# Two transformer blocks in split fp32: a third seven-product K pair in each FFN gemm, its weight sums made by an adding DMA

## The chip, the cores and the metric

The kernel runs on one core of a Trainium2 chip. The metric is the device time of one execution in microseconds (us), the median of several runs. The difference between two kernels is what counts; both compute the same function of the same inputs.

## The reference, cut to what matters

One sequence of S = 256 tokens with D = 2048 features passes through two blocks in float32, B = 1. Nearly all of the arithmetic is matrix products with weights that are used once:

```
# block 1
h = rmsnorm(x);  proj = h @ w_in                   # 2048 -> 6144
x = x + concat(dilated_attention, diff_attention) @ w_out
h = rmsnorm(x)
x = x + (silu(h @ w_gate) * (h @ w_up)) @ w_down   # 2048 -> 2 x 5632 -> 2048
x = rmsnorm(x)
# block 2
z = rmsnorm(x) @ w_in_2                            # 2048 -> 10256
merged = g_a * (fox_attention @ w_proj_a) + g_m * (mlstm @ w_proj_m)
x = x + merged @ w_out_2
u = causal_dwconv(rmsnorm(x) @ w_up_2, conv_w, conv_b)   # 2048 -> 11264
x = x + (silu(u_gate) * u_val) @ w_down_2          # 5632 -> 2048
```

## The kernel before

**Products in split fp32.** TensorE multiplies in a reduced fp32 format (F32R). Each fp32 operand is split into a high part and a low part in that format, and a product is hi·hi + hi·lo + lo·hi, three matmuls (`mm3`, L131 to L134, or L137 and L138 where the weights are the stationary operand). A weight tile goes one way through the engines: SP issues its DMA into a tile `raw` (L70, 128 x 2048, 1 MB, 3 buffers), ScalarE (ACT) casts 1024 columns of it to `wh` (L80), VectorE (DVE) subtracts to get `wl` (L81), and TensorE (PE) uses both. `wh` and `wl` have 4 buffers each.

**Gemms.** The function `gemm` (L167) makes 256 x 1024 outputs in four PSUM banks `c[t][n]`, a token half by a column half, and walks over "K pairs", 256 rows of the weight at a time. A plain pair is a 2 x 2 by 2 x 2 block product: 8 products of three matmuls with 512 columns, 24 matmuls. The first `n_sum` pairs of a gemm are done with seven products instead (a Strassen-Winograd scheme): 21 matmuls. For those, sums of blocks stand in the place of blocks. The sums of the activations are made once per pair (`sums`, L118: four 128 x 128 operations on GpSimd (POOL), a cast on ACT and a subtraction on DVE). The sums of the weights are made for each gemm: `ta` (L187, one DVE operation 128 x 1024) and `tb` (L188 and L189). After the seven-product pairs the extra banks p1, p5, p6, p7 are combined into four tiles `plus` (L212 to L216), which are added to the outputs: by POOL in `add_blocks` (L253), where the output goes into the residual, or by DVE in `block` (L243).

**Stages.** The norms' row factors are applied late, so that products can start without them. The first stage takes the transposed input `xin` from HBM, splits it (L105 to L111) and multiplies (`xstat`, L151), while POOL squares `xin` for the first norm (L403 to L410). Then come attention, the output gemms `wo1`, the squares of the residual (`sq_add`) and the transposes of the residual back into stationary form (`resid_pairs`, L289, by L263). The first FFN has three parts of 3, 4 and 4 gate-up gemms (8 K pairs each, weights `wgu`), and each part ends in two down gemms (`wd`) of 6, 8 and 8 K pairs. The second block's FFN does its up products with `conv` (L919, by `wstat`, L140) and its down gemms `wd2` in the same three parts; the row factor there is broadcast over partitions by a matmul (`bcast`, L350) at its start. Seven-product pairs stand in 11 gate-up, 6 `wd` and 6 `wd2` gemms, N_SUM = N_SUMD = 2 of them in each: 46.

**Order.** The code is not the order of the instructions: a scheduler with modelled times puts each engine's instructions in a row. On each engine they then run in that row, each waiting for the semaphores of what it reads and of the buffers it writes.

## Time and profile before

| | |
|---|---|
| median of 3 runs | 2576.76 us (2575.09 to 2577.85) |
| profiled execution | 2575.72 us |
| its span | 2573.8 us |
| TensorE busy | 2530.7 us, 98% of the span |
| weight loads of TensorE | 81% |
| VectorE busy | 71% |
| ScalarE busy | 52% |
| GpSimd busy | 7% |
| mean HBM rate | 184 GB/s |

The span is the time between the first and the last instruction of the profiled execution; 1.9 us of the measured time lie around it. A busy share is a mean over stages with different limits. Matmuls are pipelined, so that a matmul is shown as lasting 0.39 us although the next one starts 0.23 us after it: what a matmul costs is read from start to start. "Idle before", in square brackets, is the time in which an engine stood idle ahead of an instruction, with what ended it.

### The profile page before, as it was taken

The numbers are of one execution on the slowest core, as the hardware profiler recorded it, in microseconds if no ns is written. First come the engines' busy times: TensorE is split into PE (matmuls) and PEld (weight loads), VectorE is DVE, ScalarE is ACT, GpSimd is POOL, SyncE is SP. The second block draws the span as 40 slices with busy tenths as digits, with TensorE's granted clock in tenths as the row PEclk, the third lists the DMA queues.
The fourth block names the chain that finished last, engine by engine and source line by source line (L and its number), as shares of the span: only waits on it lengthen the run. The fifth ranks groups of instructions, "written<-read, shape, count | busy, mean of one in ns | idle before, by whom it ended". The sixth has DMA issues, their size and how long they took to land. (4 is left out here: it accounts for less than half of the span.)

```text
span 2573.8 us, 31105 instructions
## 1 busy us (share of the span) xinstructions
PE 2530.7 (98%) x12050; PEld 2094.5 (81%) x12050; DVE 1821.8 (71%) x2354; ACT 1340.8 (52%) x1882; POOL 167.3 (7%) x125
## 2 busy tenths in 40 slices
PE   7999999999999999999999999999899999999999
PEld 6888887878878888777888888888788888888887
DVE  6666556789778877877566555455589887878796
ACT  4555555555555454546455644444455455545553
POOL 3000000102101100110000000000000100110011
PEclk9999999999999999999999999999999999999999
DMA  7444444545545555554544455555455655555554
GB/s 273 152 158 170 171 164 158 190 176 198 209 167 210 180 210 170 197 196 165 195 161 154 176 180 188 189 195 180 154 190 180 210 183 185 192 196 184 193 178 166
DMA packets 66244, 472.60 MB, mean 184 GB/s; under 512 B 7345, under 2 KB 7601, under 8 KB 9777
## 3 DMA queue, kind: packets, MB, share of 16 engines
q1 hardware_dynamic: 65520, 468.53, 51.8%
q8 instruction: 94, 1.54, 0.2%
q10 hardware_dynamic: 576, 2.10, 0.2%
q14 instruction: 54, 0.43, 0.0%
HBM read 468.50 MB, written 2.10 MB: 183 GB/s over the span
## 5 line engine op out<-in xcount | busy, mean ns | idle before, releaser
L81 DVE TENSOR_TENSOR wl<-raw,wh 128x1024 fp32r<-128x1024 f32 (+1 forms) x882 | 1082.4, 1234 | 597.3 <-ACT wh L80 596.1
L80 ACT CAST wh<-raw 128x1024 fp32r<-128x1024 f32 (+1 forms) x882 | 902.0, 1029 | 995.1 <-PE d L134 649.5
L133 PE MATMUL d<-wl,x 128*128 128x512 f32 x1532 | 599.6, 393 | 11.6 <-DVE wl L81 11.6
L134 PE MATMUL d<-wh,x 128*128 128x512 f32 x1532 | 597.9, 392 | 0.0
L132 PE MATMUL d<-wh,x 128*128 128x512 f32 x1532 | 572.1, 394 | 3.4 <-ACT wh L80 3.2
L137 PE MATMUL a<-x,wh 128*128 128x512 f32 x1536 | 542.0, 398 | 0.0
L138 PE MATMUL a<-x,wl 128*128 128x256 f32 x1536 | 431.6, 281 | 0.0
L133 PEld LDWEIGHTS d<-wl,x 128*128 128x128 f32 x1532 | 288.4, 188 | 74.8 <-DVE wl L81 15.2
L137 PEld LDWEIGHTS a<-x,wh 128*128 128x128 f32 x1536 | 289.0, 188 | 70.1
L132 PEld LDWEIGHTS d<-wh,x 128*128 128x128 f32 x1532 | 287.1, 188 | 67.1 <-ACT wh L80 8.2
L134 PEld LDWEIGHTS d<-wh,x 128*128 128x128 f32 x1532 | 288.6, 188 | 59.1 <-DVE x L116 0.5
L138 PEld LDWEIGHTS a<-x,wl 128*128 128x128 f32 x1536 | 290.9, 189 | 0.2
L133 PE MATMUL d<-wl,y 128*128 128x512 f32 x624 | 242.2, 391 | 0.0
L134 PE MATMUL d<-wh,y 128*128 128x512 f32 x624 | 241.5, 390 | 0.0
L132 PE MATMUL d<-wh,y 128*128 128x512 f32 x624 | 217.3, 392 | 0.1
L133 PEld LDWEIGHTS d<-wl,y 128*128 128x128 f32 x624 | 117.1, 188 | 27.0 <-DVE wl L81 2.3
L132 PEld LDWEIGHTS d<-wh,y 128*128 128x128 f32 x624 | 116.5, 188 | 25.8 <-ACT wh L80 2.2
L134 PEld LDWEIGHTS d<-wh,y 128*128 128x128 f32 x624 | 117.2, 188 | 24.0
L81 DVE TENSOR_TENSOR wl<-ta,wh 128x1024 fp32r<-128x1024 f32 x46 | 56.2, 1223 | 46.6 <-ACT wh L80 46.6
L132 PE MATMUL a<-wh,y 128*128 128x512 f32 x216 | 83.4, 392 | 3.2 <-DVE x L111 3.2
L134 PE MATMUL a<-wh,y 128*128 128x512 f32 x216 | 84.4, 392 | 0.0
L133 PE MATMUL a<-wl,y 128*128 128x512 f32 x216 | 84.4, 391 | 0.0
(335 smaller groups left out, 2418.9 us busy)
## 6 DMA issues: line engine op xcount, KB each, us to landing
raw<-in_wgu SPq DMA_DIRECT2D x88, 1024.0 KB, 4.8
raw<-in_wd SPq DMA_DIRECT2D x88, 1024.0 KB, 4.8
raw<-in_wup SPq DMA_DIRECT2D x88, 1024.0 KB, 4.8
raw<-in_w SPq DMA_DIRECT2D x47, 1024.0 KB, 4.8
raw<-in_wo SPq DMA_DIRECT2D x32, 1024.0 KB, 4.8
raw<-in_wgs SPq DMA_DIRECT2D x32, 1024.0 KB, 4.8
raw<-in_wfox SPq DMA_DIRECT2D x24, 1024.0 KB, 4.8
raw<-in_wpr SPq DMA_DIRECT2D x16, 1024.0 KB, 4.8
```

What stands on the lines that cost most here:

```text
L80: act.copy(wh[:, :n], src)
L81: dve.tensor_sub(wl[:, :n], src, wh[:, :n].bitcast(F32))
L132: pe.matmul(ps, ah, wh, start=start, stop=False)
L133: pe.matmul(ps, ah, wl, start=False, stop=False)
L134: pe.matmul(ps, al, wh, start=False, stop=stop)
L137: pe.matmul(ps, wh, pr.t[:, :, j, :], start=start, stop=False)
L138: pe.matmul(ps[:, 0:S], wl, pr.hi(j), start=False, stop=stop)
```

## The change

- **Three seven-product pairs per gemm.** N_SUM and N_SUMD go from 2 to 3, 69 seven-product pairs in place of 46.
- **First weight sums by DMA.** L187 is gone. SP issues a plain DMA that writes the block b12 twice into `ta` (128 x 2 x 512, 512 KB written), and then GpSimd issues a DMA that reads the blocks b11 and b22 from HBM (512 KB) and adds them to what stands in `ta`. Both are issued for up to three seven-product pairs ahead (`ta_ahead`), over gemm bounds, into 3 buffers. The host lays the weights out as b11, b22, b12, b21, so that each DMA reads contiguous columns.
- **No elementwise work of these kinds on GpSimd.** The four operations in `sums` go to DVE. The squares of the first norm go to ACT, which reads the untransposed input `xn` (two squares of 128 x 2048). The tiles `plus` are added to the residual by DVE, ahead of the gemm's last pairs (`fold`). GpSimd keeps the 69 adding DMAs and the 8 additions of L896.
- **Pairs in turns.** In a gemm, a seven-product pair takes turns with a plain pair: `one`, the plain pair's first half, `two`, its second half, `three`. The chain that makes `plus` comes right after the last seven-product pair, and the last pair goes bank by bank.
- **Smaller raw tiles.** 128 x 1024 with 7 buffers in place of 128 x 2048 with 3: 966 rows of SP in place of 457.
- **Order around the stages.** The residual's transposes for one half of the columns are asked for right after that half's gemm, ahead of the squares. In the second FFN four `conv` products are started, half by half, ahead of the norm's row factor. A few PSUM banks and temporary tiles change places and numbers.

```diff
-N_SUM = 2
-N_SUMD = 2
-TT_BUFS = 1
+N_SUM = 3
+N_SUMD = 3
+TA_BUFS = 3
+TB_BUFS = 1
+BY_COL = ((0, 0), (1, 0), (0, 1), (1, 1))
...
-    rp = ctx.enter_context(tc.tile_pool(name="rp", bufs=3))
+    rp = ctx.enter_context(tc.tile_pool(name="rp", bufs=7))
...
-            pool.tensor_sub(f[:, 0], a21, a22)
-            pool.tensor_sub(f[:, 2], a11, a21)
-            pool.tensor_sub(f[:, 1], f[:, 0], a11)
-            pool.tensor_add(f[:, 3], a12, f[:, 1])
...
+            dve.tensor_sub(f[:, 0], a21, a22)
+            dve.tensor_sub(f[:, 2], a11, a21)
+            dve.tensor_sub(f[:, 1], f[:, 0], a11)
+            dve.tensor_add(f[:, 3], a12, f[:, 1])
...
+    def ta_ahead(k):
+
+        while len(given) < min(len(jobs), k + 3):
+            src = jobs[len(given)]
+            ta = sx.tile([P, 2, 512], F32, tag="ta", name="ta", bufs=TA_BUFS)
+            nc.sync.dma_start(ta, src[:, 1024:1536].unsqueeze(1).to_broadcast([P, 2, 512]))
+            given.append(ta)
+            if len(given) > 1:
+                ta_add()
+        while len(added) < min(len(jobs), k + 2):
+            ta_add()
+
+    def ta_add():
+        n = len(added)
+        pool.dma_start(given[n], jobs[n][:, 0:1024].rearrange("p (a b) -> p a b", a=2), accum_op=ALU.add)
+        added.append(n)
...
+            def load(self):
+                ta_ahead(len(taken))
+                self.ta = given[len(taken)]
+                taken.append(self.i)
+                self.r = [raw_tile(srcs[self.i][:, 0:1024]), raw_tile(srcs[self.i][:, 1536:2048])]
+                self.tb = sx.tile([P, 2, 512], F32, tag="tb", name="tb", bufs=TB_BUFS)
+
+            def sum_b(self):
+                dve.tensor_add(self.tb[:, 0], self.ta[:, 0], self.r[0][:, 512:1024])
+                dve.tensor_add(self.tb[:, 1], self.tb[:, 0], self.r[1][:, 0:512])
...
+            def two(self):
+                later(lambda: self.cut(2, self.ta.rearrange("p a b -> p (a b)"), 1024))
+                mm(p5, lambda: self.lhs(0), self.w[2], 0)
+                mm(p7, lambda: self.lhs(2), self.w[2], 512)
...
+        n_with = min(n_sum, max(0, len(plains) - tail))
+        if not n_sum:
+            n_with = 0
+        for i, sv in enumerate(sevens):
+            pl = plains[i] if i < n_with else None
+            later(sv.load)
+            if pl:
+                later(pl.load)
+            if pl is None:
+                later(sv.sum_b)
+            sv.one()
+            if pl:
+                later(lambda pl=pl: pl.cut(0, dve))
+                later(lambda pl=pl: pl.cut(1, dve))
+                later(sv.sum_b)
+                pl.part(0)
+            sv.two()
+            if pl:
+                pl.part(1)
+            sv.three()
...
-    def add_blocks(c, plus, g):
-
-        for t in range(2):
-            for n in range(2):
-                o = g * 1024 + n * 512
-                r = resid[:, t, o:o + 512]
-                if plus is not None:
-                    pool.tensor_add(r, r, plus[t][n])
-                dve.tensor_add(r, c[t][n], r)
+    def add_blocks(c, g):
+
+        for t, n in BY_COL:
+            o = g * 1024 + n * 512
+            r = resid[:, t, o:o + 512]
+            dve.tensor_add(r, c[t][n], r)
...
-        sqx = ap1.tile([P, 4, S], F32, tag="on", name="sqx")
-        pool.tensor_mul(sqx, xf[:, 0:4], xf[:, 0:4])
...
+        def xn2_hook():
+            ss = np_.tile([P, 2], F32, tag="ssx", name="ssx")
+            for t in range(2):
+                sq = ap1.tile([P, 2, 4, S], F32, tag="qk", name="sqx", bufs=3)
+                act.activation(sq.rearrange("p a b s -> p (a b s)"), resid[:, t], AF.Square, accum_out=ss[:, t:t + 1])
+            rl.append(rtok_from(ss, "rtok", EPS))
...
+        c, p = gemm([wo1[h][g][i] for h in range(2) for i in range(4)], y1, N_SUM1,
+                    lambda p, g=g: add_blocks(p, g), tail=2, tag="da"[g], last=BY_COL)
+        add_blocks(c, g)
+        xr += resid_pairs(g, lambda k: gain(G_FFN, k), N_SUM)
         sq_add(g)
-        xr += resid_pairs(g, lambda k: gain(G_FFN, k), N_SUM)
...
+        early = {n: bank("da"[n < FC]) for n in (0, FC, 1, FC + 1)}
+        for i in range(2):
+            for n, ps in early.items():
+                wstat(ps, wup[n], xr, halves=(i,))
+
         def conv(n):
-            ps = bank()
-            wstat(ps, wup[n], xr)
+            ps = early.pop(n, None)
+            if ps is None:
+                ps = bank()
+                wstat(ps, wup[n], xr)
+            if not rbs:
+                rbs.append(bcast(rtok_from(sq_done(), "rtok", EPS), "rb"))
+            rb = rbs[0]
...
+    a = w.reshape(k // 256, 2, P, m // 1024, 2, 512).transpose(3, 0, 2, 1, 4, 5)
+    a = a.reshape(m // 1024, k // 256, P, 4, 512)[:, :, :, [0, 3, 1, 2]]
```

Three places in the rows of instructions follow, as the scheduler leaves them.

The first is GpSimd's row at the start of the program. Before, it holds the squares of the transposed input (`sqx` and `sqi` are sums and squares, the names in brackets are semaphores of the DMAs that bring `xin`):

```order
L404 TENSOR_TENSOR sqx_283<-xin_75 128x1024 [waits DMAHW4_49,DMAHW2_49,DMAHW0_49]
L407 TENSOR_TENSOR sqi_285<-xin_75 128x1024 [waits DMAHW6_49]
L408 TENSOR_TENSOR sqx_283<-sqx_283,sqi_285 128x1024 [waits Pool_49]
L407 TENSOR_TENSOR sqi_288<-xin_75 128x1024 [waits DMAHW0_49]
L408 TENSOR_TENSOR sqx_283<-sqx_283,sqi_288 128x1024 [waits Pool_49]
```

Now the first thing in it is adding DMAs of the first gate-up gemms, which come much later in time:

```order
L186 DMA ta_3543<-in_wgu 128x1024 [waits DMAHW0_49,DVE_49,DMAHW5_49,PE_49,Activation_49]
L186 DMA ta_3545<-in_wgu 128x1024 [waits DMAHW6_49]
L186 DMA ta_3548<-in_wgu 128x1024 [waits DMAHW7_49]
L186 DMA ta_3641<-in_wgu 128x1024 [waits DMAHW2_49,DMASW0_49,DVE_49]
L186 DMA ta_3724<-in_wgu 128x1024 [waits DMAHW7_49,DMASW1_49,DVE_49]
```

What moved: nothing of GpSimd lies beside the first stage any more, and an adding DMA waits for its plain DMA (a DMAHW semaphore) at the head of GpSimd's row.

The second place is VectorE's row at the first `wd` gemm, of 6 K pairs. Before, a sum `ta` waits for the DMA of its raw tile, and the subtraction of the sum (`wl<-ta`) follows:

```order
L187 TENSOR_TENSOR ta_4713<-raw_4711 128x1024 [waits DMAHW2_49]
L81 TENSOR_TENSOR wl_4668<-raw_4661,wh_4667 128x1024 [waits Activation_49]
L188 TENSOR_TENSOR tb_4714<-ta_4713,raw_4711 128x512 [waits DVE_49]
L189 TENSOR_TENSOR tb_4714<-tb_4714,raw_4711 128x512 [waits DVE_49]
L81 TENSOR_TENSOR wl_4719<-raw_4711,wh_4718 128x512 [waits Activation_49]
L81 TENSOR_TENSOR wl_4726<-ta_4713,wh_4725 128x1024 [waits Activation_49]
```

Now `tb` waits for the adding DMA of its `ta` (a DMASW semaphore). `ta_4744`, which the last row reads, has the buffer that `wl_4713<-ta_4371`, the first row, releases:

```order
L84 TENSOR_TENSOR wl_4713<-ta_4371,wh_4712 128x1024 [waits Activation_49]
...
L231 TENSOR_TENSOR tb_4751<-ta_4454,raw_4747 128x512 [waits DMASW2_49,DVE_49]
...
L84 TENSOR_TENSOR wl_4772<-ta_4454,wh_4771 128x1024 [waits Activation_49]
...
L231 TENSOR_TENSOR tb_4798<-ta_4661,raw_4794 128x512 [waits DMASW3_49,DVE_49]
...
L362 TENSOR_TENSOR xin_75<-s1_4838,xin_75 128x512 [waits Activation_49]
...
L231 TENSOR_TENSOR tb_4959<-ta_4744,raw_4955 128x512 [waits DMAHW5_49,DMASW4_49,DVE_49]
```

What moved: between that release and that reader 15 VectorE instructions stand, 8 with 1024 columns and 7 with 512; the plain and the adding DMA of `ta_4744` have to be done in the time of these.

The third place is TensorE's row where the second FFN begins (`m` are the operands of the last `wo2` gemm). Before, all 16 transposes and the matmul of `bcast` (`a<-dg,ones`) stand between the last `wo2` product and the first up product:

```order
L134 MATMUL d<-wh,m 128x512
L263 MATMUL a<-cst_t,xin 128x128 x16
L355 MATMUL a<-dg,ones 128x256
L137 MATMUL a<-x,wh 128x512
L138 MATMUL a<-x,wl 128x256
```

Now up products stand between the transposes:

```order
L137 MATMUL d<-wh,m 128x512
L371 MATMUL a<-cst_t,xin 128x128 x2
L140 MATMUL d<-x,wh 128x512
L141 MATMUL d<-x,wl 128x256
L140 MATMUL d<-x,wh 128x512
L141 MATMUL d<-x,wl 128x256
...
L371 MATMUL a<-cst_t,xin 128x128 x8
L140 MATMUL d<-x,wh 128x512
L141 MATMUL d<-x,wl 128x256
...
L463 MATMUL a<-dg,ones 128x256
```

What moved: the matmul of `bcast` comes after all the four early `conv` products, 64 K steps of two matmuls.

## Rows read from the trace of the kernel before

**Rows 1.** The page's first part: busy time, share of the span and number of instructions of each engine.

```profile
PE 2530.7 (98%) x12050; PEld 2094.5 (81%) x12050; DVE 1821.8 (71%) x2354; ACT 1340.8 (52%) x1882; POOL 167.3 (7%) x125
```

**Rows 2.** The timeline of TensorE in the first FFN: start, duration, engine, line, operation.

```profile
702.02 0.39 PE L132 MATMUL d<-wh,x 128*128 128x512 f32 x1
702.25 0.39 PE L133 MATMUL d<-wl,x 128*128 128x512 f32 x1
702.47 0.39 PE L134 MATMUL d<-wh,x 128*128 128x512 f32 x1
```

**Rows 3.** The timeline of the start, of GpSimd, VectorE, ScalarE and TensorE.

```profile
7.79 1.89 POOL L404 TENSOR_TENSOR sqx<-xin 128x1024 f32<-128x1024 f32 x1 [7.35 <-DMA xin<-in_xT]
...
25.95 3.03 POOL L410 TENSOR_TENSOR sqx<-sqx 128x512 f32<-128x512 f32 x2
...
11.65 9.17 DVE L111 SCALAR_TENSOR_TENSOR x<-xin,x 128x256 fp32r<-128x256 f32 x4
20.74 6.22 DVE L81 TENSOR_TENSOR wl<-raw,wh 128x1024 fp32r<-128x1024 f32 x2
...
16.93 1.99 ACT L80 CAST wh<-raw 128x1024 fp32r<-128x1024 f32 x2 [0.19 <-DMA raw<-in_w]
...
23.70 0.80 PE L133 MATMUL d<-wl,x 128*128 128x512 f32 x1 [8.72 <-DVE wl L81]
24.29 0.63 PE L134 MATMUL d<-wh,x 128*128 128x512 f32 x1
...
27.71 0.50 PE L134 MATMUL d<-wh,x 128*128 128x512 f32 x1
```

**Rows 4.** Groups of VectorE instructions by line and shape over the whole span: count, busy time, mean ns of one, idle time before them.

```profile
L187 DVE TENSOR_TENSOR ta<-raw 128x1024 f32<-128x1024 f32 x46 | 56.6, 1230 | 5.3 <-DMA raw<-in_wgu 2.7 <-DMA raw<-in_wd 2.7
L254 DVE TENSOR_TENSOR xin<-d,xin 128x512 f32<-128x512 f32 x60 | 39.9, 687 | 15.8 <-PE d L134 15.8
L81 DVE TENSOR_TENSOR wl<-raw,wh 128x512 fp32r<-128x512 f32 x49 | 33.7, 688 | 20.7 <-ACT wh L80 20.7
L188 DVE TENSOR_TENSOR tb<-ta,raw 128x512 f32<-128x512 f32 x46 | 31.7, 688 | 0.7
L111 DVE SCALAR_TENSOR_TENSOR x<-a,gp_t,x 128x256 fp32r<-128x256 f32 x28 | 12.0, 476 | 0.7 <-ACT x L110 0.7
```

**Rows 5.** The timeline of TensorE, ScalarE and VectorE at the start of the first gate-up gemm.

```profile
424.88 0.66 PE L263 MATMUL a<-cst_t,xin 128*128 128x128 f32 x4 [1.67 <-ACT sv L281]
426.22 0.66 PE L263 MATMUL a<-cst_t,xin 128*128 128x128 f32 x4 [0.68 <-ACT sv L281]
430.37 0.79 PE L132 MATMUL d<-wh,sx 128*128 128x512 f32 x1 [2.08 <-ACT sx L127]
437.74 0.50 PE L133 MATMUL a<-wl,sx 128*128 128x512 f32 x1 [0.77 <-DVE wl L81]
...
422.78 0.63 ACT L339 ACTIVATE sq<-xin 128x512 f32<-128x512 f32 x1
...
422.11 1.22 DVE L81 TENSOR_TENSOR wl<-raw,wh 128x1024 fp32r<-128x1024 f32 x1
423.24 1.22 DVE L81 TENSOR_TENSOR wl<-tb,wh 128x1024 fp32r<-128x1024 f32 x1
```

**Rows 6.** The timeline of TensorE where the last `wd` gemm's first half of outputs has been added and transposed.

```profile
1120.67 0.77 PE L132 MATMUL a<-wh,y 128*128 128x512 f32 x1 [3.25 <-DVE x L111]
```

**Rows 7.** The timeline of TensorE at the start of the second FFN.

```profile
1836.35 1.19 PE L355 MATMUL a<-dg,ones 128*128 128x256 f32 x2 [6.97 <-DVE dg L353]
1837.98 0.63 PE L137 MATMUL a<-x,wh 128*128 128x512 f32 x1
1838.62 0.63 PE L137 MATMUL a<-x,wh 128*128 128x512 f32 x1
...
1841.18 0.39 PE L137 MATMUL a<-x,wh 128*128 128x512 f32 x1
1841.53 0.39 PE L137 MATMUL a<-x,wh 128*128 128x512 f32 x1
```

**Rows 8.** Windows: from and to, length, busy time of PE, PEld, DVE, ACT and POOL (instructions), granted clock of TensorE (1 is 2.4 GHz), share of the DMA engines, GB/s. The first is the start, the second the start of the first gate-up gemm, the third a stretch of the first FFN with a 6-pair `wd` gemm, the fourth the start of the second FFN, the last most of the two 6-pair `wd2` gemms.

```profile
0.00:30.00 30.00, 17.20 (x61) 12.74 (x62) 24.09 (x19) 15.55 (x26) 19.96 (x13) 0.83 0.62 229
421.00:439.00 18.00, 12.80 (x60) 9.40 (x59) 15.53 (x28) 16.43 (x34) 5.26 (x8) 0.81 0.17 58
573.00:617.00 44.00, 43.49 (x191) 34.79 (x191) 42.35 (x44) 24.08 (x27) 11.91 (x7) 1.00 0.61 212
1820.00:1842.00 22.00, 15.03 (x70) 12.47 (x69) 11.31 (x21) 11.03 (x24) 0.00 (x0) 0.84 0.40 141
1975.00:2036.00 61.00, 60.77 (x265) 48.92 (x264) 56.42 (x58) 30.71 (x34) 13.98 (x8) 1.00 0.59 205
```

**Rows 9.** GpSimd's additions to the residual: count, busy time, mean ns of one.

```profile
L253 POOL TENSOR_TENSOR xin<-xin,e 128x512 f32<-128x512 f32 x12 | 26.9, 2240 | 10.6 <-DVE e L216 10.6
```

**Rows 10.** DMA issues: queue, count, KB of each, median us from issue to landing.

```profile
raw<-in_wd SPq DMA_DIRECT2D x88, 1024.0 KB, 4.8
out<-xin ACTq DMA_DIRECT2D x4, 512.0 KB, 2.6
gp_t<-in_gp SPq DMA_DIRECT2D x1, 357.5 KB, 8.4
```

More of the change, by code (lines that the diff above doesn't have):

```diff
@@ L67, in raw_tile @@
     def raw_tile(src):
-        t = rp.tile([P, 2048], F32, tag="raw", name="raw")
+        t = rp.tile([P, 1024], F32, tag="raw", name="raw")
         n = src.shape[-1]
@@ L153, in xstat @@
         for q in range(4):
-            raw = pre[q] if q < len(pre) else raw_tile(src4[q])
+            raw = pre[q] if q < len(pre) else [raw_tile(src4[q][:, h * 1024:(h + 1) * 1024]) for h in range(2)]
             if then and q in then:
@@ new lines, in gemm @@
+        sevens = [Seven(i) for i in range(n_sum)]
+        plains = [Plain(i) for i in range(n_sum, nk)]
+        leads, plains = plains[:lead], plains[lead:]
+        for pl in leads:
+            later(pl.load)
[10 more added lines that the diff above has]
+            if pl:
+                later(pl.load)
+            if pl is None:
+                later(sv.sum_b)
+            sv.one()
+            if pl:
+                later(lambda pl=pl: pl.cut(0, dve))
+                later(lambda pl=pl: pl.cut(1, dve))
+                later(sv.sum_b)
+                pl.part(0)
+            sv.two()
+            if pl:
+                pl.part(1)
+            sv.three()
@@ L216, in gemm @@
             dve.tensor_sub(e22, p5, u3)
[L217 to L233 removed]
+            return fold([[s1, u4], [u3, e22]])
+        tails = plains[n_with:]
+        if n_sum:
+            later(lambda: plus_.append(chain()))
+            if mid:
+                later(mid)
+        plus_ = []
+        for i, pl in enumerate(tails):
+            later(pl.load)
+            later(lambda pl=pl: pl.cut(0, dve))
+            later(lambda pl=pl: pl.cut(1, dve))
+            if i == len(tails) - 1:
+                pl.by_bank()
+            else:
+                pl.part(0)
+                pl.part(1)
+            if mid and not n_sum and i == min(1, len(tails) - 2):
+                later(mid)
+        for f in todo:
+            f()
+        return c, plus_[0] if plus_ else None
+    ET_BUFS = 8
     def et(name):
@@ L372, in run_late @@
             late.pop(0)()
-    raw0 = rp.tile([P, 2048], F32, tag="raw", name="raw")
+    raw0 = [rp.tile([P, 1024], F32, tag="raw", name="raw") for i in range(2)]
     for a, b in ((0, 1), (1, 2), (2, 4), (4, 8), (8, 12), (12, 16)):
@@ L386, in body @@
         elif a in (4, 8):
-            first.append(raw_tile(w1[0][a // 4]))
+            first.append([raw_tile(w1[0][a // 4][:, h * 1024:(h + 1) * 1024]) for h in range(2)])
     y1 = []
@@ L564, in body @@
                     ypair(y1).put(h % 2, ps[:, :S], g08[:, 0:1])
-        for g in range(2):
-            c, p = gemm([wo1[h][g][i] for h in range(2) for i in range(4)], y1, 0, None, "da"[g])
-            add_blocks(c, p, g)
     sctx = ExitStack()
-    sx = sctx.enter_context(tc.tile_pool(name="sx", bufs=max(1, N_SUM)))
+    sx = sctx.enter_context(tc.tile_pool(name="sx", bufs=1))
+    for pr in y1[:N_SUM1]:
+        v = et("sv")
+        dve.tensor_add(v, pr.t[:, 0].rearrange("p j s -> p (j s)").bitcast(F32),
+                       pr.t[:, 1].rearrange("p j s -> p (j s)").bitcast(F32))
+        pr.sums("sy", v.rearrange("p (j s) -> p j s", j=2))
     xr = []
@@ L579, in body @@
     dve.tensor_mul(gg, gp_t[:, G_FINAL:G_FINAL + 16], gp_t[:, G_N1:G_N1 + 16])
+    for ga, gb in PARTS:
+        jobs += [wgu[gi][i] for gi in range(ga, gb) for i in range(N_SUM)]
+        jobs += [wd[g][2 * ga + i] for g in range(2) for i in range(N_SUMD)]
+    ta_ahead(0)
     xn_ = []
@@ L601, in body @@
         for g in range(2):
[L602 to L603 removed]
+            c, p = gemm([wd[g][2 * ga + i] for i in range(n_pairs)], hs, N_SUMD, lambda p, g=g: add_blocks(p, g), run_late, tail=2, last=BY_COL)
+            add_blocks(c, g)
             if part == len(PARTS) - 1:
+                xn_ += resid_pairs(g, lambda k: gg[:, k:k + 1], 0)
                 sq1_add(g)
[L606 removed]
     xr = xn_
@@ L952, in body @@
             for g in range(2):
-                c, p = gemm([wd2[g][2 * ga + i] for i in range(n_pairs)], hs, N_SUMD)
-                add_blocks(c, p, g)
+                c, p = gemm([wd2[g][2 * ga + i] for i in range(n_pairs)], hs, N_SUMD, lambda p, g=g: add_blocks(p, g), last=BY_COL)
+                add_blocks(c, g)
                 if part == len(PARTS) - 1:
```

180 lines of the change are left out of this document (90 added, 90 removed).

## The prediction

> **What bounds the kernel now.** I read the page's first part first: TensorE is busy 98% of the span, VectorE 71%, GpSimd 7% [rows 1]. So TensorE's matmuls set the time nearly everywhere, and a change can win in two ways: fewer matmuls, or less idle time and half-speed time of TensorE at the few places where it waits. The TensorE timeline of a quiet stretch gives the price of a matmul with 512 columns from start to start: 702.02, 702.25, 702.47, or 0.227 us [rows 2] (the 0.39 us shown as duration overlaps the next). Then I looked for waits. They stand in four places: the start, where TensorE idles 8.72 us for VectorE [rows 3]; the first gate-up gemm, with four waits [rows 5]; the transposes after a last `wd` gemm, 3.25 us [rows 6]; and the start of the second FFN, 6.97 us [rows 7]. The windows show that these places also lose clock: 0.81 to 0.84 of 2.4 GHz granted on average, against 1.00 in the quiet ones [rows 8]. After a wait the matmuls stand 0.43 us apart (24.29 on), which is the 1.2 GHz level [rows 3]. Third, the stretches with 6-pair down gemms: there VectorE is busy 56.42 of 61 us and 42.35 of 44 [rows 8], so VectorE is nearly a second bound in just those.
>
> **Term A, matmuls.** 46 seven-product pairs become 69. Each of the 23 new ones saves 3 matmuls: 69 x 0.227 = -15.6 us [rows 2]. All of it lies on the path, as TensorE is the bound.
>
> **Term B, the start.** GpSimd squares `xin` from 7.79 to 29 us [rows 3]. Beside it VectorE needs 9.17 us for four 128 x 256 operations, against 0.476 each later [rows 4], and 6.22 us for two subtractions that take 1.22 each [rows 3, 5]. VectorE's row there is the same in both kernels; with GpSimd silent, these six should take 4 x 0.48 + 2 x 1.22 = 4.4 us instead of 15.4. ACT had the next raw tile at 16.93 with an idle time of 0.19 us for its DMA, so the transfers follow at once with another wait, though a short one [rows 3]. I leave 0.7 us of the 8.72: -8.0. From 24.29 to 27.71 stand 8 matmuls, 0.43 apart; at 0.227 they save 1.6. Together -9.6 us. The squares go to ACT: four operations of 512 columns take about 0.62 us each [rows 5], so two of 2048 columns take at most 8 x 0.62 = 5.0 us of an engine that is 52% busy [rows 1]. The factor that they give is needed for the rotation of q and k, with the k and v products still to run; I take 0, at worst 5.0.
>
> **Term C, the first gate-up gemm.** The waits sum to 1.67 + 0.68 + 2.08 + 0.77 = 5.2 us [rows 5]; some six matmuls that follow at half speed, 0.43 apart as at the start, cost 6 x 0.2 = 1.2 (the window's clock is 0.81 [rows 8]). Now half the transposes stand inside the second `wo1` gemm, and the operations of `sums` are done by VectorE. Something of the chain ACT, VectorE, ACT remains for the second half: I keep 1.4 and take -5.0 us.
>
> **Term D, after the last wd gemm.** The 3.25 us for `x` [rows 6] come from VectorE having sums and subtractions of the next gemm ahead of the transposes' results. Columns are now finished first and turned before the squares: -3.3 us with the half-speed matmuls behind it paying for what is left.
>
> **Term E, the second FFN.** The wait of 6.97 us is a serial chain (squares, factor, diagonal, `bcast`) that TensorE stands still for [rows 7]. In the new row, 64 K steps of up products stand ahead of that matmul, each 0.35 us at full clock (41.18 to 41.53), 22 us in all, longer than the chain: -7.0. Five steps of 0.64 instead of 0.35 [rows 7] go too: -1.4. Sum -8.4 us.
>
> **Term F, VectorE.** This is what the change pays. A seven-product pair needs three operations of 1.22 us and three of 0.69 (one subtraction, two for `tb`), 5.75 us, once `ta` is gone [rows 4, 5]; a plain pair two of 1.23, 2.46. The chain has four of 0.68, 2.7, and the residual takes eight of 0.687, 5.5, of which four were GpSimd's [rows 4]. A 6-pair gemm so costs 3 x 5.75 + 3 x 2.46 + 2.7 + 5.5 = 32.9 us of VectorE, against (63 + 72) x 0.227 = 30.6 of TensorE: 2.3 too much in each of four such gemms. But durations overstate: two subtractions back to back start 1.13 apart, not 1.22 (422.11 and 423.24) [rows 5]; by that ratio, 0.926, it is 30.5 and no loss. The 8-pair ones have 37.8 against 183 x 0.227 = 41.5. So the bounds are 0 and +9.2, nothing below 0, since TensorE is the bound; I take +1 in each, **+4 us**, as both ends are near.
>
> **Term G, the adding DMA.** Nothing in the trace shows one. Its lower bound is its bytes at the rate of the windows, 205/0.59 = 347 GB/s [rows 8]: 512 KB in 1.5 us of all engines. Other bounds: 2.6 us, the landing of the stores of 512 KB, and 12 us, if it went as badly as the 8.4 us for the 357.5 KB of `gp_t` [rows 10]. I take 3.0 us, twice the lower one, since it must read its target too, and near the stores' row. A 6-pair gemm moves, beside it, 3 x 1280 + 3 x 1024 KB = 7.08 MB, 20.4 us; with 3 x 3.0 it is 29.4 of 30.6. It just fits; the 8-pair gemms (26.4 + 9.0 of 41.5) have room. For latency: a `ta` buffer is released 8 x 1.23 + 7 x 0.69 = 14.7 us ahead of its next reader where that is tightest, 13.6 by spacing, and a plain and an adding DMA of 4.8 us landing each [rows 10] fit. What stands behind an adding DMA that waits for its plain one is only other adding DMAs. Cost 0; upper end as in the slow rival and beyond. VectorE waits at `tb` if it comes late, and everything behind it: the subtractions that feed TensorE.
>
> The Trainium skill, "SBUF — State Buffer", section "SBUF: two separate sides", says that VectorE and GpSimd share a port pair that one of them holds for a whole instruction. The start's rows agree (0.48 us becomes 2.3) [rows 3]. The same section warns that VectorE can keep GpSimd from writing the descriptors of a DMA that GpSimd issues; the second rival is this. Its "who interferes with whom" excepts operations of two tensors, by inference only, and most of VectorE's here are of that kind.
>
> **Sum.** Against the profiled execution's 2575.72: -15.6 - 9.6 - 5.0 - 3.3 - 8.4 + 4 = -37.9, or 2537.8. The median lies 1.04 above the profiled execution: **2539 us**.
>
> **Rivals.** *Gaps re-form (13%).* The waits of C, D and E are ends of chains through ACT and VectorE, and TensorE may wait as long for the next link. Against it: early up products cover more time than the chain. Only A and B stay: 2575.7 - 15.6 - 9.6 + 1.0 = 2551.5.
>
> *Descriptors starved (7%).* VectorE delays each adding DMA, and waits for it in turn. Priced by the longest mean of a GpSimd operation beside VectorE, 2.24 us [rows 9], three times a gemm: 6.7 us. By spacing, the 8-pair gemms and gate-up gemms hide it; the 6-pair ones, with VectorE at its bound, lose 6.6 each, 26 in all: 2575.7 - 41.9 + 26.5 + 1.0 = 2561.
>
> *Slow adding DMA (8%), slower than before.* If it holds the engines a us, transfers become the bound of the 6-pair gemms from a = 3.4, (30.6 - 20.4)/3, of the 8-pair ones from 5.0, and of the gate-up gemms (about 43.3 us with their transposes) from 5.6. At a = 6.0 it is 7.8 x 4 + 2.9 x 8 + 1.1 x 11 = 66.5 us: 2575.7 - 41.9 + 66.5 + 1.0 = 2601. It wins back nothing from about a = 5.6, near four times the plain price. For it: an adding DMA has two reads for a write. Against: a stores' row of 2.6 us.
>
> *Small transfers (2%).* Raw tiles of 512 KB; if each held the engines for its 2.6 us of landing [rows 10], a 6-pair gemm's 13.5 of them would take 35 us, and the time would pass 2700. Against it: the start moves 229 GB/s at a share of 0.62, 369 GB/s at full share, with many loads below 1 MB [rows 8]. The Trainium skill, "DMA: Bandwidth & Descriptors", section "Bandwidth", asks for 1 MiB or more in a transfer; by its rule this rival would hold.
>
> **Numbers.** The forecast has 70%. Its own range is 2522 (F at 0, all of C, and the small waits elsewhere too) to 2552 (F at +9, the factor's 5). The range, 2520 to 2566, takes in the first two rivals and leaves out the slow ones. A measurement of this kernel tells some 0.2%, 5 us, from no change. Faster: 70 + 13 + 6 = 89%; same: 2%; slower: 9%, the slow transfers and the far end of the starved one.
>
> **What would show it.** Right: TensorE matmuls 0.227 apart and 69 fewer of them; no wait over 1 us between 14 and 30 us; no 7 us gap in front of the second FFN's up products, with `bcast` behind 64 K steps; VectorE over 95% busy in the 6-pair gemms with TensorE idle by about 1 us each. Wrong: VectorE idle ahead of `tb<-ta` for a DMA, a DMA share near 1 in those gemms (slow adding), GpSimd's DMA issues long beside VectorE (starved), or new waits of TensorE for `sx`, `x` or `dg`.

## The result: 2515.9 us, and the profile after

The changed kernel takes 2515.85 us (median of 4 runs, 2514.97 to 2519.18), the one before 2576.64: 60.8 us less, a ratio of 0.9767 (95% interval 0.975 to 0.9784). The forecast was 2539, its range 2520 to 2566: the direction was right, the gain 23 us larger than forecast and the time below the range.

The page's first part, answering to [rows 1]. TensorE, now at 99%, is still the bound; GpSimd has nearly nothing left.

```profile
PE 2498.6 (99%) x11977; PEld 2081.7 (83%) x11977; DVE 1830.0 (73%) x2538; ACT 1386.2 (55%) x1943; POOL 74.1 (3%) x81
```

To see where the time went, I cut both traces at the same events and took the lengths (us). "First product on sums" is the first matmul with the stationary operand `sx`; the first FFN's end is its last down product, block 2's its last `wo2` product, the second FFN's its last down product.

| stretch | before | after | difference | of it predicted |
|---|---|---|---|---|
| waits and slow matmuls in the first 50 us | 15.5 | 6.7 | -8.9 | -9.6 (B) |
| the rest up to the first product on sums (430.37, now 413.64) | | | -7.9 | -5.0 (C) |
| first FFN | 731.8 | 699.8 | -32.0 | -12.9 (51 of A's matmuls -11.6, D -3.3, F +2) |
| block 2 up to `wo2` | 665.0 | 665.3 | +0.3 | 0 |
| second FFN | 741.8 | 730.0 | -11.8 | -10.5 (18 of A's matmuls -4.1, E -8.4, F +2) |

Eight transposes and three products, some 1.6 us, stood ahead of the first product on sums and stand behind it now; otherwise the stretches hold the same work, but for the matmuls of A. The missing 23 us are mainly in the first FFN, 19 of them. The windows show it in one view (from and to, length, busy time of PE, PEld, DVE, ACT, POOL, granted clock, DMA share, GB/s). A quiet 200 us stretch of it before, away from all four places that the prediction listed:

```profile
640.00:840.00 200.00, 197.33 (x875) 160.63 (x875) 159.21 (x172) 101.28 (x114) 14.76 (x12) 1.00 0.56 196
```

And after: the same stretch, the start, the two 6-pair `wd` gemms and the two 6-pair `wd2` gemms, answering to [rows 8].

```profile
0.00:30.00 30.00, 25.58 (x99) 20.50 (x100) 18.59 (x28) 20.68 (x31) 0.20 (x4) 0.94 0.93 348
...
550.00:615.00 65.00, 64.25 (x281) 51.39 (x280) 61.26 (x75) 36.27 (x41) 5.17 (x6) 1.00 0.90 267
...
1920.00:1980.00 60.00, 57.76 (x251) 46.31 (x250) 53.53 (x65) 33.33 (x38) 4.32 (x5) 1.00 0.83 250
...
640.00:840.00 200.00, 200.00 (x899) 165.57 (x898) 171.29 (x206) 114.70 (x132) 11.54 (x15) 1.00 0.84 255
```

899 matmuls and transposes stand in these 200 us instead of 875, with VectorE and the transfers much busier than before, and TensorE never waits. In the two 6-pair stretches it does.

The start after (start, duration, engine, line, operation), answering to [rows 3]. The four operations of 9.17 us take 1.66; what TensorE waits for now is ACT, and ACT a DMA.

```profile
10.27 1.04 ACT L83 CAST wh<-raw 128x1024 fp32r<-128x1024 f32 x1 [1.34 <-DMA raw<-in_w]
...
11.37 0.73 PE L135 MATMUL d<-wh,x 128*128 128x512 f32 x2 [2.38 <-ACT wh L83]
...
12.49 1.66 DVE L114 SCALAR_TENSOR_TENSOR x<-xin,x 128x256 fp32r<-128x256 f32 x4
```

The start of the second FFN, answering to [rows 7]: the first up product follows the transposes at once, and `bcast`'s matmul stands 24 us later, without a wait.

```profile
1779.13 0.48 PE L140 MATMUL d<-x,wh 128*128 128x512 f32 x1
...
1802.99 0.59 PE L463 MATMUL a<-dg,ones 128*128 128x256 f32 x2
```

The DMA queues (packets, MB, share of 16 engines) and the issues of the sums (count, KB, median us to landing). q0 is GpSimd's: 8.0% of 2514.3 us is 201 us, or 2.9 us of all 16 engines for each of the 69 adding DMAs. The prediction took 3.0.

```profile
q1 hardware_dynamic: 147648, 486.65, 56.5%
q0 software_dynamic: 9936, 36.18, 8.0%
...
ta<-in_wd SPq DMA_DIRECT2D x36, 512.0 KB, 7.5
ta<-in_wd POOLq DMA_DIRECT2D x36, 512.0 KB, 8.5
```

One place became worse, the start of block 2. VectorE scales the residual by the final norm, four operations in a row, ahead of a subtraction that TensorE waits for; then come slow matmuls.

```profile
1129.87 4.86 DVE L738 SCALAR_TENSOR_TENSOR xin<-xin,r,gf 128x1024 f32<-128x1024 f32 x4
1134.66 1.22 DVE L84 TENSOR_TENSOR wl<-raw,wh 128x1024 fp32r<-128x1024 f32 x1
...
1135.93 0.50 PE L136 MATMUL d<-wl,x 128*128 128x512 f32 x1 [1.95 <-DVE wl L84]
...
1136.57 0.63 PE L136 MATMUL d<-wl,x 128*128 128x512 f32 x1
1137.00 0.63 PE L137 MATMUL d<-wh,x 128*128 128x512 f32 x1
```

### The profile page after: what moved, and what is told of

Read it like the earlier page. It is cut to its first block, busy times and chain, and to the rows that moved or that the text cites. A ratio compares the mean times of both kernels' runs of the same rounds, so it can differ in the third digit from the quotient of the medians.

```text
span 2514.3 us, 32725 instructions
## 1 busy us (share of the span) xinstructions
PE 2498.6 (99%) x11977; PEld 2081.7 (83%) x11977; DVE 1830.0 (73%) x2538; ACT 1386.2 (55%) x1943; POOL 74.1 (3%) x81
## 4 chain that ended last, share of the span: by engine, by line
PE 98%; DVE 1%; issue 0%; DMA 0%; ACT 0%; SPq 0%; DVEq 0%; ACTq 0%
PE d L136 20%; PE d L137 20%; PE d L135 20%; PE a L140 14%; PE a L141 7%; PE a L135 4%; PE a L136 4%; PE a L137 4%; PE a L371 1%; PE a L571 1%; DVE wl L84 0%; PE a L578 0%; PE d L140 0%; DMA raw<-in_w 0%; PE a L630 0%
## 5 line engine op out<-in xcount | busy, mean ns | idle before, releaser
L84 DVE TENSOR_TENSOR wl<-raw,wh 128x1024 fp32r<-128x1024 f32 (+1 forms) x882 | 1037.0, 1181 | 557.4 <-ACT wh L83 554.0
L136 PE MATMUL d<-wl,x 128*128 128x512 f32 x1466 | 575.3, 393 | 2.5 <-DVE wl L84 2.5
L137 PE MATMUL d<-wh,x 128*128 128x512 f32 x1466 | 574.1, 392 | 0.0
L135 PE MATMUL d<-wh,x 128*128 128x512 f32 x1466 | 528.2, 394 | 3.5 <-ACT wh L83 3.5
L135 PEld LDWEIGHTS d<-wh,x 128*128 128x128 f32 x1466 | 276.1, 189 | 61.8 <-ACT wh L83 4.7
L136 PEld LDWEIGHTS d<-wl,x 128*128 128x128 f32 x1466 | 276.0, 188 | 61.2 <-DVE wl L84 4.0
L137 PEld LDWEIGHTS d<-wh,x 128*128 128x128 f32 x1466 | 276.2, 188 | 56.2
L136 PE MATMUL d<-wl,y 128*128 128x512 f32 x552 | 213.1, 390 | 1.2 <-DVE wl L84 1.2
L137 PE MATMUL d<-wh,y 128*128 128x512 f32 x552 | 212.3, 390 | 0.0
L135 PE MATMUL d<-wh,y 128*128 128x512 f32 x552 | 175.6, 391 | 0.2 <-ACT wh L83 0.2
L136 PEld LDWEIGHTS d<-wl,y 128*128 128x128 f32 x552 | 103.6, 188 | 23.6 <-DVE wl L84 2.0
L135 PEld LDWEIGHTS d<-wh,y 128*128 128x128 f32 x552 | 103.4, 188 | 22.1 <-ACT wh L83 0.6
L137 PEld LDWEIGHTS d<-wh,y 128*128 128x128 f32 x552 | 103.4, 188 | 21.5 <-DVE y L119 0.2
L84 DVE TENSOR_TENSOR wl<-ta,wh 128x1024 fp32r<-128x1024 f32 x69 | 84.2, 1220 | 4.8 <-ACT wh L83 4.6
```

Of the source, the lines that this page charges most:

```text
L84: eng.tensor_sub(wl[:, :n], src, wh[:, :n].bitcast(F32))
L135: pe.matmul(ps, ah, wh, start=start, stop=False)
L136: pe.matmul(ps, ah, wl, start=False, stop=False)
L137: pe.matmul(ps, al, wh, start=False, stop=stop)
```

## The experiments

All runs edit the changed kernel, if nothing else is said. The kernel before was run again beside each of them and took 2578.1 to 2579.9 us, against 2576.6 in the result; the ratios are to these. Differences below some 3 us are therefore read from the traces, by place. "Waits and slow matmuls" is the time by which the steps from one matmul's start to the next are longer than those of the same shapes elsewhere in the trace.

### The third pair and the turns

**two_sevens**: N_SUM = N_SUMD = 2. 

> The changed kernel with two seven-product pairs per gemm instead of three, turns, DMAs and all else kept. Term A of the prediction: 69 matmuls more at 0.227 us, 2515.9 + 15.6 = 2531.5 us, with no new waits in the first FFN. Rival (the third pair itself took the small waits ahead of the second group of transposes away): these come back in 11 gate-up gemms at about 1 us each, 2542 us.

**no_turns** and **two_no_turns** (the latter with the two constants as well):

```diff
-        n_with = min(n_sum, max(0, len(plains) - tail))
+        n_with = 0
```

> The changed kernel with the three seven-product pairs one after the other and the plain pairs behind them. If the turns removed the small waits of the first FFN (about 1.0 us in each of 11 gate-up gemms before): 2515.9 + 11 = 2527 us, with waits again at the second group of transposes. Rival (turns are not needed, since three pairs in a row keep the two groups of transposes apart as well): within 3 us of 2516.

> The changed kernel with two seven-product pairs and no turns: in TensorE's row the two groups of four transposes then stand 4 matmuls apart as before, against 27 or more in the two other kernels. If the distance of these groups is what the small waits hang on: 15.6 us for the matmuls and about 11 us for the waits, 2542 us, with waits of 0.6 us and a slow restart at the second group. Rival (the waits went because GpSimd no longer works beside VectorE, or by the DMA sums): 2531.5 us, no waits.

Measured: two_sevens 2522.9 us (ratio 0.9781, 0.9764 to 0.9797), no_turns 2578.9 (0.9998, 0.9989 to 1.0008), two_no_turns 2553.5 (0.9902, 0.9887 to 0.9917). The turns are the largest part of the change: without them its whole gain is gone, and with two pairs they are worth 31 us. The rest of the change, with two pairs and no turns, is worth 26 us. For no_turns the forecast missed by 52 us, because I had not thought of the wait that follows below. The third pair is worth only 7 us with turns and costs 25 without them. My 15.6 us for it hold for the matmuls alone; the traces show what is taken back: two_sevens has no waits in the 6-pair gemms, and its first FFN, block 2 and second FFN have 2.3, 3.3 and 3.5 us less of waits and slow matmuls.

The same 200 us window in two_sevens, no_turns and two_no_turns, one row for each:

```profile
640.00:840.00 200.00, 200.00 (x899) 165.53 (x898) 156.16 (x179) 105.55 (x119) 7.76 (x9) 1.00 0.76 228
```

```profile
640.00:840.00 200.00, 194.06 (x849) 154.15 (x848) 159.86 (x195) 106.05 (x122) 11.22 (x13) 1.00 0.78 242
```

```profile
640.00:840.00 200.00, 197.78 (x881) 161.49 (x880) 149.15 (x174) 101.07 (x114) 6.91 (x8) 1.00 0.70 224
```

In part, what waits in two_no_turns is what waited before: the second group of four transposes in a gate-up gemm, which needs the PSUM bank of the first group, and so ACT's cast and VectorE's subtraction of that group (five such places; at most others TensorE waits for an ACT cast). Before there are eight of them, as at 530.23, and three waits for a cast, as at 486.14:

```profile
528.22 0.60 PE L263 MATMUL a<-cst_t,h 128*128 128x128 f32 x4
...
530.23 0.66 PE L263 MATMUL a<-cst_t,h 128*128 128x128 f32 x4 [0.47 <-DVE y L116]
...
486.14 0.50 PE L132 MATMUL a<-wh,sx 128*128 128x512 f32 x1 [0.90 <-ACT wh L80]
```

and in two_no_turns:

```profile
517.12 0.33 PE L371 MATMUL a<-cst_t,s 128*128 128x128 f32 x1 [0.47 <-DVE y L119]
```

TensorE also waits again, for VectorE's `x`, at two of the four places that the prediction listed: behind the first product on sums (C) and in the last down gemm, where the first half of outputs is transposed (D):

```profile
422.62 0.77 PE L135 MATMUL a<-wh,x 128*128 128x512 f32 x1 [1.99 <-DVE x L114]
...
1108.16 0.47 PE L135 MATMUL a<-wh,y 128*128 128x512 f32 x1 [1.14 <-DVE x L114]
```

Together with the waits and slow matmuls beside them they cost 5.1 and 4.8 us in two_no_turns, 5.4 and 5.8 in no_turns, and nothing in the changed kernel and in two_sevens.

In no_turns something else waits, in the row of seven-product pairs itself. VectorE's second sum for `tb`, ACT's cast of it and TensorE's product follow each other in a chain (L232 at 636.00, cast at 636.77, matmul at 637.87). VectorE's subtraction from `tb` waits for the cast as well (637.85), and only behind it can the next pair write `tb`, as there is one buffer:

```profile
636.00 0.68 DVE L232 TENSOR_TENSOR tb<-tb,raw 128x512 f32<-128x512 f32 x1
...
636.77 1.05 ACT L83 CAST wh<-tb 128x1024 fp32r<-128x1024 f32 x1 [1.00 <-DVE tb L232]
...
637.85 1.23 DVE L84 TENSOR_TENSOR wl<-tb,wh 128x1024 fp32r<-128x1024 f32 x1 [1.17 <-ACT wh L83]
...
631.40 0.50 PE L135 MATMUL a<-wh,sx 128*128 128x512 f32 x1 [0.56 <-ACT wh L83]
...
637.87 0.50 PE L135 MATMUL a<-wh,sx 128*128 128x512 f32 x1 [0.54 <-ACT wh L83]
```

From one pair to the next it is 637.87 - 631.40 = 6.47 us, where 21 matmuls need 4.8. Two runs tell this chain from VectorE's mere amount of work.

**no_turns_two_tb**: no_turns with `bufs=2` for `tb` in the first FFN and ET_BUFS 6 to make room. 

> The kernel without turns (2578.9 us), with two buffers for tb in the first FFN (and two temporary tiles less to make room). If one buffer and its round trip make the waits in a row of seven-product pairs: most of the 58 us of the first FFN goes, 2530 us. Rival (VectorE's work in such a row, 5.3 us by spacing in each pair against 4.8 of TensorE, sets the pace): at most a third goes, 2560 us or more.

**no_turns_no_tb**: no_turns without the two additions of `sum_b`, the third part casting `ta` once more. 

> The kernel without turns, without the two additions that make tb: the third part takes the first sums again in their place, so the outputs of the seven-product pairs are not the reference's. VectorE's work falls to 4.4 us in each pair, and no link from VectorE's sum over ScalarE to TensorE is left. If VectorE's work or this link makes the waits, they go: 2516 to 2525 us. Rival (the casts, the raw tiles or the adding DMAs are late in a row of seven-product pairs): 2560 us or more.

Measured: 2540.1 us (0.9846, 0.9831 to 0.9861) and 2512.2 (0.9737, 0.9722 to 0.9751). With a second buffer, the waits and slow matmuls of the first FFN fall from 58 to 15 us, and the window is full (VectorE as busy as with turns); the second FFN, which kept one buffer, keeps 15 of its 17 us. So it is mostly the round trip over one buffer, not VectorE's amount of work. Without the sums the second FFN has no waits left and the first some 7 us, all at the places of C and D.

```profile
640.00:840.00 200.00, 200.00 (x898) 165.53 (x897) 171.33 (x207) 116.22 (x133) 11.21 (x13) 1.00 0.81 250
```

### The sums by DMA, and GpSimd's other work

**sum_on_dve**: `ta` by VectorE, no adding DMAs; b12 then comes once, with the raw tiles.

```diff
+                dve.tensor_add(self.ta, self.r[0].rearrange("p (a b) -> p a b", a=2),
+                               r1[:, 0:512].unsqueeze(1).to_broadcast([P, 2, 512]))
```

> The changed kernel with the first weight sums made by VectorE again (69 operations of 1.23 us) and no adding DMAs. By term F, VectorE then has 36.6 us by durations, 33.9 by spacing, in each 6-pair gemm against 30.6 of TensorE: 3.3 x 4 = 13 us more, 2529 us; the 8-pair and gate-up gemms hide it. Rival 1 (durations count, not spacing): 24 us more, 2540 us. Rival 2 (the adding DMAs themselves held the gemms up, and their absence pays for VectorE's work): 2516 us or less.

**pool_sums**: `sums` and the `plus` additions by `pool` again. 

> The changed kernel with the activations' sums and the additions of the plus tiles to the residual on GpSimd again (84 and 48 operations). VectorE is relieved of some 56 us of work in all, but GpSimd's operations slow VectorE's beside them. By the prediction, which priced this shift at nothing outside the 6-pair gemms: -4 to 0 us, 2514 us. Rival (GpSimd beside VectorE was behind waits in the first FFN): +5 us or more, 2521 us or above.

Measured: 2538.1 us (0.984, 0.9826 to 0.9855) and 2522.2 (0.9783, 0.9768 to 0.9798). The DMA sums are worth 22 us. The number is near the bound by durations (24), but not for its reason. In the trace the first FFN is 21.1 us longer and the second 5.5. From the first to the last down product the two 6-pair `wd` gemms take 70.6 us against 64.4, the two `wd2` ones 70.3 against 64.8: 12 us, as the bound by spacing had it (13). The other 15 us stand in the gate-up and 8-pair gemms of the first FFN, which by the forecast hide this work. In the window away from the 6-pair gemms VectorE is busy 91% of the time and TensorE waits 1.4 us; in all of the first FFN behind the 6-pair gemms it waits 6.3:

```profile
640.00:840.00 200.00, 198.65 (x886) 162.59 (x885) 182.94 (x217) 111.92 (x128) 0.00 (x0) 1.00 0.60 196
...
613.00:1134.00 521.00, 514.73 (x2279) 419.69 (x2279) 473.81 (x558) 291.08 (x339) 0.00 (x0) 1.00 0.59 196
```

pool_sums costs 6 us, of which 5.5 in the first FFN's waits. VectorE has 132 instructions fewer than in the changed kernel and is busy longer, 1842.2 us against 1830.0: less work for it was no gain.

### The start, the order and the early products

**pool_squares**: `sqx` by `pool` again, as at L403 to L410, in place of ACT's squares. 

> The changed kernel with the first norm's squares on GpSimd again, beside the first products. Term B of the prediction: VectorE slows down as before, TensorE waits some 8 us and runs the next matmuls at half speed: 2515.9 + 9 = 2525 us, all of it in the first 30 us. Rival (the start is bound by its transfers now, whose share of the DMA engines rose to 0.93 in the first 30 us): within 3 us of 2516.

**squares_first**: `sq_add` (and `sq1_add`) ahead of `resid_pairs` in three places. 

> The changed kernel with the residual's squares asked for ahead of its transposes in all three places, as before. Terms C and D: part of the waits at the first gate-up gemm (8.8 us with slow matmuls before) and after the last down gemm (4.9 us) returns, while the new wait in front of block 2 (about 4.6 us with slow matmuls) may go: +5 us, 2521 us. Rival (the scheduler places both by its own times, and the order of the code is worth nothing): 2516 us.

**no_early_up**: `early = {}`, and the row factor made and broadcast at once. 

> The changed kernel without the four early up products, the row factor made and broadcast ahead of them. Term E: the wait of 7 us and the slow matmuls behind it return: 2515.9 + 9 = 2525 us. Rival (turning each half's columns ahead of the squares already shortened the chain): 3 to 5 us, 2520 us.

Measured: 2538.8 (0.9847, 0.9832 to 0.9861), 2516.0 (0.9761, 0.9744 to 0.9777) and 2523.1 us (0.9782, 0.9768 to 0.9797). squares_first has the same gaps as the changed kernel, block 2's among them, but it is a weak test: the scheduler moved ACT's squares at one place only, ahead of the first FFN (364 to 369 us). At the last down gemms and ahead of the second FFN no row of ACT or VectorE differs, so the order of the squares was not tested there. The early products are worth 7 us; without them the old wait is back:

```profile
1783.86 1.19 PE L463 MATMUL a<-dg,ones 128*128 128x256 f32 x2 [6.36 <-DVE dg L461]
```

The squares on GpSimd bring the old start back, as forecast:

```profile
11.85 9.15 DVE L114 SCALAR_TENSOR_TENSOR x<-xin,x 128x256 fp32r<-128x256 f32 x4
...
23.88 0.80 PE L136 MATMUL d<-wl,x 128*128 128x512 f32 x1 [8.88 <-DVE wl L84]
```

But this kernel lost 23 us, not 9. The rest lies in both FFNs and block 2, whose instructions are the changed kernel's. There matmuls with `sx`, `sy` or `m` as stationary operand start 233 ns apart, as in the kernel before; in the changed kernel they start 227 ns apart.

### The addresses

Before: six steps from 1825.83 to 1827.23, 1.40 us, 233 ns each. After: six steps in 1.36 us, 227 ns each.

```profile
1825.83 0.39 PE L134 MATMUL d<-wh,m 128*128 128x512 f32 x1
...
1827.23 0.40 PE L134 MATMUL d<-wh,m 128*128 128x512 f32 x1
```

```profile
1776.95 0.39 PE L135 MATMUL d<-wh,m 128*128 128x512 f32 x1
...
1778.31 0.39 PE L135 MATMUL d<-wh,m 128*128 128x512 f32 x1
```

The clock is granted in full in both. The built programs differ in where tiles lie. The change's squares on ACT need one small tile more (`ssx`), and what is allocated behind it begins 32 bytes further on within its 64. First byte of a buffer within its 64 bytes of SBUF:

| kernel | `x`, `y`, `wh`, `wl` | `sx`, `sy`, `m` | products on `m` |
|---|---|---|---|
| before | 32 | 0 | 233 ns |
| changed | 32 | 32 | 227 ns |
| pool_squares | 32 | 0 | 233 ns |

**pad_sums**, **pad_all** and **before_pad** add one unused tile, in the pool of small tiles, ahead of all tiles, and in the kernel before; the order of TensorE's instructions stays the same.

```diff
+    np_.tile([P, 2], F32, tag="pad", name="pad")
```

> The changed kernel with one unused tile of 8 bytes more in the pool of small tiles; every instruction and its order stay. All tiles behind it move by 32 bytes: the stationary sums sx and sy and the operands m now begin at a multiple of 64 bytes, as in the kernel before, x, y, wh and wl stay 32 bytes off one. If the address sets the spacing (matmuls on sx, sy, m start 233 ns apart before, 227 ns after, and 233 again in the run with GpSimd's squares, which has one small tile less): 1212 such matmuls x 6.4 ns = 7.8 us, and some of their neighbours, 2524 to 2528 us. Rival (the spacing comes from GpSimd's work or from the order): 2516 us.

> The changed kernel with one unused tile of 8 bytes more ahead of everything, order unchanged: now x, y, wh, wl, sx, sy and m all begin at a multiple of 64 bytes. If what counts is that the stationary and the moving tile begin alike in their 64 bytes: 2516 us. Rival (a stationary tile at a multiple of 64 bytes is slow whatever the moving one does): over 8000 matmuls x 6.4 ns, 2567 us or more.

> The kernel before with one unused tile of 8 bytes more, order unchanged: sx, sy and m move to 32 bytes off a multiple of 64, as in the changed kernel. If the address sets the spacing, this part of the change's gain is had alone: 936 matmuls x 6.4 ns = 6.0 us and their neighbours, 2570 us. Rival: 2576.6 us.

**pool_squares_pad** adds it to pool_squares. 

> The changed kernel with GpSimd's squares again, and an unused small tile that puts sx, sy and m back on the addresses that they have in the changed kernel. If the run without it (2538.8 us) was slower by two things, 9 us of VectorE's slowness at the start and 12 us of addresses: 2525 us. Rival (GpSimd's work at the start slows matmuls later in another way): 2538 us.

Measured: pad_sums 2526.5 us (0.9793, 0.9778 to 0.9807), pad_all 2514.2 (0.9745, 0.973 to 0.9759), before_pad 2574.2 against 2579.1 (0.9978, 0.9969 to 0.9987), pool_squares_pad 2526.1 (0.9793, 0.9777 to 0.981). pad_sums has the six steps at 1.40 us again, pad_all at 1.36:

```profile
1785.10 0.40 PE L136 MATMUL d<-wh,m 128*128 128x512 f32 x1
...
1786.50 0.40 PE L136 MATMUL d<-wh,m 128*128 128x512 f32 x1
```

```profile
1775.89 0.39 PE L136 MATMUL d<-wh,m 128*128 128x512 f32 x1
...
1777.25 0.39 PE L136 MATMUL d<-wh,m 128*128 128x512 f32 x1
```

With both operands at 32 or both at 0 the spacing of these products is 227 ns; with the stationary one at 0 and the moving one at 32 it is 233. In the kernel before this costs 5 us (3 to 8 by the interval), 46 x 12 + 384 = 936 matmuls x 6.4 ns = 6.0 by the estimate; it is a part of the change's gain that no line of the diff intends. In the changed kernel, with more such products, it would cost 11 (pad_sums). pool_squares splits into 10 us of squares and 13 of addresses.

A like difference stays open. In the first part of the second FFN a `conv` step (512 columns with `wh`, then 256 with `wl`) takes 347 ns in the kernel before and in no_early_up, and 353 ns in all other runs, before_pad among them. For 384 such steps that is 2.6 us: a loss of the change, and before_pad's second FFN is longer by as much. The weights and `x` begin alike in all of these runs, so the table does not explain it.

### Two versions from the runs

**four_and_scale**: N_SUM = 4 with ET_BUFS 6, two pairs in the 6-pair down gemms, and the scaling of block 2's start (L738 in the changed kernel) moved into the loop of the `wgs` gemms, 512 columns of the residual at a time. 

> A version made from the runs: four seven-product pairs in the gate-up gemms (11 x 3 matmuls less, -7.5 us), two in the four 6-pair down gemms, whose new waits the third pair does not pay (about +2.7 of matmuls, -5 of waits), two temporary tiles less to make room, and the four scalings of the residual by the final norm moved from in front of block 2 to its gate gemms (the wait and slow matmuls there, -4 us): 2502 us. Rival (VectorE, with 41 us by durations against 40.8 in the gate-up gemms, becomes their bound): 2515 us or more.

**three_and_scale**: the same with N_SUM = 3 and ET_BUFS 8. 

> The last version with three seven-product pairs in the gate-up gemms instead of four, and its temporary tiles back. The scalings moved out of block 2's start bring 5.0 us by the trace of the last version, two pairs in the 6-pair gemms of both FFNs 3 us: 2515.9 - 8 = 2508 us. Rival (the fourth pair in the gate-up gemms pays for its waits): above the 2512.2 us of that version.

Measured: 2512.2 us (0.9737, 0.9721 to 0.9754) and **2507.2 us** (0.9717, 0.9703 to 0.9732), the fastest of all. A fourth pair does not pay: the first FFN gets 14.0 us of waits and slow matmuls, the changed kernel 2.6, three_and_scale 0.2. The fourth pair of a gate-up gemm has no plain pair left to take turns with, and VectorE is busy 92% of the window from 640 us; which of the two makes the waits no run separates. Block 2 is 5 us shorter, and its start and the two 6-pair `wd2` gemms are now full:

```profile
1120.00:1140.00 20.00, 20.00 (x91) 16.08 (x90) 15.81 (x36) 16.21 (x30) 0.00 (x0) 1.00 0.55 184
1920.00:1980.00 60.00, 60.00 (x275) 49.95 (x274) 50.83 (x59) 31.20 (x34) 3.46 (x4) 1.00 0.87 260
```

## Why the prediction was right and wrong

**What bounds the kernel: the step that failed.** "They stand in four places" was wrong. In the first FFN of the kernel before, the wait of 0.47 us with its slow restart stands at the second group of transposes in eight gemms, 1.0 us each by the steps from start to start, and a longer one, 1.7 us, in the second gate-up gemm of each of the three parts; a 200 us window of TensorE at 197.33 shows it. The prediction names them once, as "the small waits elsewhere too" in the lower end of its own range, where they are some 11 of the 17 us below the forecast; in the sum it puts them at nothing and gives no reason. two_no_turns has such waits and two_sevens has not: the turns removed them. "Pairs in turns" was the one part of the change that I gave no term at all, neither for the waits that it takes away nor for those that a third pair in a row would have made. Some 13 of the 19 us missed in the first FFN are such waits (8 x 1.0 and 3 x 1.7). Most of the rest is 2.6 for addresses (34 pairs x 12 x 6.4 ns), 2.3 for that part of C which stands behind the first product on sums, and 1.6 for D.

**A, matmuls.** -15.6 us is right for TensorE's work, and 69 fewer matmuls are there. As the worth of the third pair it is too much: 7 us with turns, since the waits of the 6-pair gemms (F) and of block 2's start take back 9.

**B, the start.** -8.9 against -9.6, and the squares alone, with the addresses held, cost 10 us. Right, in its mechanism too.

**C and D.** Their waits are gone whole, 8.8 us with their slow matmuls for C and 4.9 for D, where I took 5.0 and 3.3. Ahead of the first product on sums nothing waits in any run of the changed kernel, with turns or without: this part of C is as forecast, though no run takes its cause apart. The rest of C and all of D hang on the turns, for which I had no term: in the four runs without them 3 to 6 us are back at each of the two places. That D comes from the order of the squares, as I argued, is not shown: squares_first left that place as it was.

**E, the second FFN.** The mechanism is as forecast. The wait and its slow matmuls fell by 9.2 in the trace against 8.4. Without the early products 7 us come back: the wait is 6.36 us instead of 6.97, and the `conv` steps are 2.6 us shorter in that run.

**F, VectorE.** +4 us for four gemms; the trace has 2.5 us of waits in the first FFN and 3.5 in the second, all in the 6-pair gemms. Right in size. By the same spacing sum_on_dve should have cost 13 us, all in the 6-pair gemms; it cost 12 there. What was wrong is that the other gemms hide VectorE's work: the first FFN's lost 15 more.

**G, the adding DMA.** 3.0 us of the engines taken, 2.9 measured, a share of 0.90 and 0.83 in the windows of the 6-pair gemms. Twice the lower bound was a choice between bounds, so that it came so near is luck in part. VectorE did wait at `tb<-ta`, ten times and 12.3 us in all, but for a plain DMA of `raw` by the profile, and TensorE waits for nothing in the 30 us behind any of these. None of the rivals came: *slow adding DMA* and *small transfers* fall by that row and by a window of 0.93 at the start; *descriptors starved* by GpSimd's issue time, 0.87 us each, and by full windows of TensorE.

**Not foreseen:** the wait of block 2's start, 2.7 us more than before; the addresses, -5 by before_pad (2.5 of them in block 2, which so stays as it was); and the longer `conv` steps, +2.6.

The forecast fell short because a gain was counted only where a wait was long enough to be seen alone. *Gaps re-form* held at one place, block 2's start; its sum left out F's +4, with which it would have been 2555.5.

## What to carry to other kernels

Sum up TensorE's time over a long quiet window before listing its waits: 1% missing there can be worth more than any one of the long waits on the list, and it lies in a chain that repeats. Work that needs a round trip over another engine and one buffer is covered by putting independent products between its links, or by a second buffer; here that was worth more than the matmuls saved. When a kernel gets faster or slower where its instructions did not change, compare the tiles' addresses, and pad one tile to test it.

## What the runs showed of the hardware that was not expected

Among products on sums and on `m`, a matmul with 512 columns started 227 ns after the one before where the stationary and the moving tile began alike within 64 bytes (both at 32, both at 0), and 233 ns after it where the stationary one began at 0 and the moving one at 32. A stationary tile at 32 with a moving one at 0, and other distances, weren't tried, and why it is so the runs don't show.

GpSimd's multiplications and additions, with both operands in SBUF, slowed VectorE's four operations from 1.66 to 9.15 us, at the same place of the same order. Its adding DMAs did nothing of the kind: in the changed kernel VectorE's subtraction of 128 x 1024 took 1219 ns in the mean beside an issue of one (50 of them), 1223 ns with GpSimd silent, and 1472 ns beside the eight products of two tensors that GpSimd kept (6 of them). The Trainium skill, "SBUF — State Buffer", section "SBUF: two separate sides", lets only one of the two engines at a time hold a shared port pair, for a whole instruction; the first row agrees. Its warning that VectorE can keep GpSimd from writing a DMA's descriptors did not show: VectorE was busy 86% of the window from 640 us, GpSimd's issues took 0.87 us in the mean and TensorE waited for none of them. Most of VectorE's operations there work on two tensors, the kind that the prediction names as the excepted one; the trace agrees with the exception, and no run here tries the other kinds.
